# Gate and output projections of a float32 transformer layer in passes of 512 columns, half of them with sums of weight blocks

## The chip, the cores and the metric

The kernel runs on one core of a Trainium2 chip. The metric is device time in microseconds, the median of several executions. Engines are named TensorE (PE in the profile; PEld are its loads of stationary blocks), VectorE (DVE), ScalarE (ACT), GpSimd (POOL) and SyncE (SP, whose queue issues most DMA transfers). A *product* below is one TensorE instruction: a stationary 128 x 128 block of one operand, times a moving block of 128 x 256 of the other, added into a PSUM bank (a bank holds 128 x 512 float32; there are eight).

## The reference

One layer on 256 tokens of width 2048, float32: gated linear attention, then a squared-ReLU MLP, then a last norm. Cut to what matters:

```python
proj = rmsnorm(x, gla_norm) @ w_in                 # q, k, v, r, g_low
q, k, v, r, g_low = split(proj)                    # 1024, 1024, 2048, 2048, 16 columns
o = chunk_causal_linear_attention(q, k, v, gate(g_low))      # 4 heads, chunks of 64
o = o * rsqrt(mean(o * o) + EPS) * o_norm
h = x + (o * silu(r)) @ w_out                      # the gate r and the output projection
a = relu(rmsnorm(h, mlp_norm) @ w_up)
h = h + (a * a) @ w_down
out = rmsnorm(h, final_norm)
```

## The kernel before, in words

**Products.** Every operand of a large projection is split into a high part (rounded to the format that TensorE takes at full rate) and a low part (the rest), and a block product is three products: high x high, high x low, low x high. ScalarE makes high parts (a cast), VectorE low parts (a subtraction). Weights come from memory by SyncE's queue into a raw room, are split into a slot, and are used from there.

**The mixer.** `natural` (line 151) makes a projection for 1024 columns: over 16 blocks of 128 input rows, and both halves of the tokens (t), the stationary block is 128 x 128 of the activations, the moving ones are the weights' columns. That is 24 products a step, 384 a pass, with four banks as sums. `weights` (128) loads and splits one step's 128 x 1024 weights. The order of passes is: values first half, keys, queries (`turned`, 169), values second half (513), gate r first half (568), second half (581), output first half (602), second half (612). `attend` (522) runs beside the first gate pass; `gate_out` (545) multiplies the normed attention output `on` by silu of the gate; `turn` (553) transposes `on` or the new h on TensorE in float32 and splits the result, four times in all: `on` twice, h twice, the last one inside the MLP's plan. `put_v` (336) writes the values' high and low parts out of a pass's banks. Side work is handed out between steps by `pump`, and a scheduler with a timeline model sets the final order of these instructions on each engine.

**Placing of blocks.** The stationary and the moving operand of a product are kept at different places modulo 256 bytes: activations start OFF = 48 words (192 bytes) into a room whose start is a multiple of 256. Behind each group of float32 transposes the kernel runs 24 products whose two operands begin at the same place modulo 256 on purpose (`xe`, `order_of`, the chunks named in SAME, 747).

**The MLP.** Its order is fixed by hand: `at(time, run)` puts steps on a plan whose unit is one product, and the plan is recorded sorted by time (1020). Each *double* is 512 x 512 weights (1 MB). An up double is 48 products. Of the down projection seven eighths go by a scheme in which four block products of a 2 x 2 arrangement are replaced by seven products with sums and differences of blocks: in `raws` (910) 24 products on raw weight blocks, in `summed` (918) 18 on sums of weight blocks, 42 in place of 48. The sums are three adds on VectorE (`adds`, 941), a high part on ScalarE (`high`, 947, two casts) and a low part on VectorE (`low`, 951). One of the sums is made by an accumulating transfer that POOL issues on the raw room (937). The activation side's differences are made by `differ` (798). `combine` (966) adds the pieces up. The chunks' splits are placed by `place_chunks` (717) ahead of their use: a high part 67 to 75 units, a low part 50 to 56 units. All eight banks go round in a list, `banks`.

```python
941        def adds():
943            add(sums[:, 0], view[:, :, 1, left], view[:, :, 0, left])
944            add(sums[:, 1], sums[:, 0], view[:, :, 0, right])
945            sub(sums[:, 2], sums[:, 0], view[:, :, 1, right])
955        at(p - 68, adds)
956        at(q - 74, lambda: high(slice(0, 2)))
958        at(q - 54, low)
959        at(p, lambda: raws(d))
960        at(q, lambda: summed(d))
```

Of the kernel before, what the change touches and what calls it, by code (L numbers as in the profile page):

```python
# [32 lines left out]
P = 128  # L33
# [34 lines left out]
SAME_R = 3  # L68
SAME_O = 3, 3
# [3 lines left out]
def tile_gla_mlp(ctx, tc, x, xt, w_vg, w_in, w_gate, w_out, w_up, w_down, final_norm, out):  # L73
# [6 lines left out]
    mixer = ExitStack()  # L80
    later = mixer.enter_context(tc.tile_pool(name="later", bufs=2))
    mid = mixer.enter_context(tc.tile_pool(name="mid", bufs=1))
    vals = mixer.enter_context(tc.tile_pool(name="vals", bufs=2))
    wpool = mixer.enter_context(tc.tile_pool(name="wpool", bufs=5))
# [199 lines left out]
    h = const.tile([P, NT, D], F32, name="h")  # L284
# [227 lines left out]

    acc = natural(row_x, rows(w_in, 3 * KEYW), G, HALF, order=order_of(SAME_V))
    flush()
    for t in range(NT):
        for c in range(2):
            put_v(acc[t][c], 512, t, G + 512 * c)


    on = later.tile([P, NT, D], F32, tag="C", name="on")  # L520

    def attend(hd, t):
        o = aux_bank()
        blocks = [(0, 0)] if t == 0 else [(0, P), (1, T)]
        vs = slice(hd * DV, (hd + 1) * DV)
        n = 0
        for src, lo in blocks:
            a_h, a_l = (a[hd][:, lo : lo + P] for a in (ath, atl))
            for s, v in ((a_h, vh), (a_h, vl), (a_l, vh)):
                halves(o, s, v[:, src, vs], n == 0, n == 3 * len(blocks) - 1)  # L530
                n += 1
        ss = st.tile([P, 1], F32, tag="oss", name="oss")
        sq = tmp.tile([P, DV], F32, tag="t512", name="sq", bufs=3)
        nc.scalar.activation(sq, o, AF.Square, scale=r1k[:, t : t + 1], accum_out=ss)
        nc.vector.tensor_scalar(ss, ss, 1.0 / DV, EPS, op0=ALU.mult, op1=ALU.add)
# [4 lines left out]
    side.extend([lambda: None] + [lambda hd=hd, t=t: attend(hd, t) for hd in range(HEADS) for t in range(NT)])  # L540


    oth = otl = None

    def gate_out(acc, c0):
        for t in range(NT):
            for c in range(2):
                lo = c0 + 512 * c
                s = tmp.tile([P, 512], F32, tag="t512", name="sr", bufs=3)
                nc.scalar.activation(s, acc[t][c], AF.Silu, scale=r1[:, t : t + 1])  # L550
                nc.vector.tensor_tensor(on[:, t, lo : lo + 512], on[:, t, lo : lo + 512], s, op=ALU.mult)

    def turn(src, row, gain, qs, banks=None):
        banks = banks or [aux_bank(), aux_bank()] + acc_banks(2)
        for q, b in zip(qs, banks):
            for i in range(2):
                kt = 2 * q + i
                for t in range(NT):
                    nc.tensor.transpose(b[:, i * T + t * P : i * T + (t + 1) * P], src[:, t, kt * P : (kt + 1) * P], ident)  # L559
        for n, i, m in ((n, i, m) for n in (0, 2) for i in range(2) for m in range(2)):  # L560
            kt = 2 * qs[n + m] + i
            s = banks[n + m][:, i * T : (i + 1) * T]
            dh, dl = row(kt)
            nc.scalar.activation(dh, s, AF.Copy, scale=gain(kt))
            nc.vector.scalar_tensor_tensor(dl, s, gain(kt), dh.bitcast(F32), op0=ALU.mult, op1=ALU.subtract)


    acc = natural(plain_x, rows(w_in, 4 * KEYW), G, HALF)
    flush()
    gate_out(acc, 0)  # L570
    oth, otl = (vals.tile([P, KT * T + 128], F32R, tag="B", name="ot" + i) for i in "hl")

    def row_o(kt):
        c = kt * T + (OFF if kt < EVEN else 64 if kt == EVEN else OFF + 64)
        return [a[:, c : c + T] for a in (oth, otl)]

    gain_o = lambda kt: go(kt % 4)
    four = lambda *a: [lambda qs=qs: turn(*a, qs) for qs in (range(4), range(4, 8))]
    turns = four(on, row_o, gain_o)
    side.extend([nothing, nothing, turns[0]])  # L580
    acc = natural(row_x, rows(w_in, 5 * KEYW), G, HALF, order=order_of(SAME_R))
    flush()
    gate_out(acc, G)


    side.extend([nothing, nothing, turns[1]])
    hs = const.tile([P, NT, 4], F32, name="hs")

    def add_h(acc, c0):
        for t in range(NT):  # L590
            for c in range(2):
                lo = c0 + 512 * c
                nc.vector.tensor_tensor(h[:, t, lo : lo + 512], acc[t][c], h[:, t, lo : lo + 512], op=ALU.add)

    def ssq_h(c0):
        for t in range(NT):
            for c in range(2):
                lo = c0 + 512 * c
                sq = tmp.tile([P, 512], F32, tag="t512", name="sq", bufs=3)
                nc.scalar.activation(sq, h[:, t, lo : lo + 512], AF.Square, accum_out=hs[:, t, lo // 512 : lo // 512 + 1])  # L600

    acc = natural(row_o, rows(w_out, 0), G, HALF, order=order_of(SAME_O[0]))
    flush()
    add_h(acc, 0)
    hth, htl = (turnp.tile([P, KT * ROW + 64], F32R, tag="A" + i, name="h" + i) for i in "hl")
    turned_h = [hth, htl]
    hth, htl = (a[:, : KT * T].rearrange("p (k t) -> p k t", t=T) for a in turned_h)
    row_h = lambda kt: [a[:, kt, :] for a in (hth, htl)]
    turns = four(h, row_h, g2)
    side.extend([nothing, nothing, turns[0]])  # L610
    side.append(lambda: ssq_h(0))
    acc_o = natural(row_o, rows(w_out, G), G, HALF, order=order_of(SAME_O[1]))
    flush()
    mixer.close()
    mlp = ctx.enter_context(tc.tile_pool(name="mlp", bufs=1, reuse_waits="tile"))

    def room_for(n, name, dtype=F32):
        return mlp.tile([P, n], dtype, tag=name, name=name)

    SLOTS, PLACE = 3, 2 * G + 64  # L620
    raw_u = [room_for(2 * G, f"rawu{i}") for i in range(2)]
    slot = [[room_for(PLACE, f"{x}{i}", F32R) for x in ("high", "low")] for i in range(SLOTS)]
    raw_d = [room_for(2 * G, f"rawd{i}") for i in range(2)]
    sums = room_for(6 * T, "sums").rearrange("p (f b c) -> p f b c", f=3, b=2)
    sums_to = [room_for(6 * T, "sums" + i, F32R).rearrange("p (f b c) -> p f b c", f=3, b=2) for i in "hl"]
    kept = room_for(12 * T, "kept").rearrange("p (c f s) -> p c f s", c=4, f=3)
    flat_forms = room_for(2 * G, "forms")
    forms = flat_forms.rearrange("p (b f s) -> p b f s", b=2, f=8)
    FORMS = 7
    spare = [a[:, KT * T :] for a in turned_h]  # L630
    acts = [
        [
            [(spare[i] if n == b == 0 else room_for(FORMS * P + (OFF if n + b + i == 4 else 64), f"act{n}{b}{i}", F32R))[:, OFF : OFF + FORMS * P] for i in range(2)]
            for b in range(2)
        ]
# [508 lines left out]
```

## Time and profile before

| what | value |
|---|---|
| median of 3 runs | 1048.14 us (1048.13 to 1048.32) |
| the profiled execution | 1048.66 us, of which its span is 1046.9 us |
| granted TensorE clock | 0.999 |
| TensorE busy | 1038.8 us of the span, 9098 instructions |
| VectorE, ScalarE, POOL busy | 811.6, 664.6, 81.7 us |
| read from memory | 206.92 MB, 200 GB/s over the span |

The span is the time from the first to the last instruction that the profiler saw; the execution's own time holds 1.8 us more around it. A line of a group gives source line, engine, operation, output <- inputs, shape and count, then busy time in us and the mean length of one in ns, then the engine's idle time just before such instructions and what ended it. The chain of work is followed back from the last instruction: at each piece to what released it. A matmul's end is modelled, so the distance between starts, which the chain's pieces give, is the better measure of a product's price.

### The profile page before, as it was taken

The page shows a single profiled execution, that of the slowest core. Times are in us where ns is not written, and L with a number is a line of the kernel's source. Part 1 is how long each engine was busy: PE and PEld are TensorE (multiplying, and loading weights), DVE is VectorE, ACT ScalarE, POOL GpSimd, SP SyncE. Part 2 cuts the span into 40 slices and gives each one's busy share as a digit, 9 for nine tenths or more (in the row PEclk, how much of TensorE's full clock was granted, in tenths as well). Part 3 has the DMA queues.
Part 4 walks back from the last instruction along what each step waited for, and adds up shares of the span by engine and source line. Part 5 has one row for each costly group of instructions (what it writes and reads, how often), then busy time and mean ns, then how long its engine had stood idle before and what let it go on. Part 6 is the DMA issues. An engine that isn't in the chain of part 4 may idle for free.

```text
span 1046.9 us, 21360 instructions
## 1 busy us (share of the span) xinstructions
PE 1038.8 (99%) x9098; PEld 1038.6 (99%) x9098; DVE 811.6 (78%) x830; ACT 664.6 (63%) x806; POOL 81.7 (8%) x97
## 2 busy tenths in 40 slices
PE   9999999999999999999999999999999999999997
PEld 9999999999999999999999999999999999999997
DVE  6668654656465566889989989989999999899894
ACT  7675544546455444667677676777767767768763
POOL 0000000010000001010101011010101111010000
PEclk9999999999999999999999999999999999999999
DMA  9857665555655555788878778787788788787662
GB/s 342 309 168 210 195 200 146 177 160 164 200 182 182 202 197 180 224 248 239 231 224 240 225 223 258 214 249 225 226 237 237 212 248 243 203 258 227 195 217 82
DMA packets 108095, 225.08 MB, mean 215 GB/s; under 512 B 6576, under 2 KB 21936, under 8 KB 107872
## 3 DMA queue, kind: packets, MB, share of 16 engines
q1 hardware_dynamic: 91664, 206.75, 60.7%
q0 software_dynamic: 15232, 14.68, 9.0%
q10 hardware_dynamic: 1104, 2.29, 0.6%
q8 instruction: 71, 1.16, 0.4%
q14 instruction: 24, 0.20, 0.0%
HBM read 206.92 MB, written 2.10 MB: 200 GB/s over the span
## 4 chain that ended last, share of the span: by engine, by line
PE 98%; issue 1%; ACT 0%; DVE 0%; POOLq 0%; POOL 0%; ACTq 0%
PE acc L149 28%; PE acc L900 22%; PE aux L774 18%; PE acc L774 16%; PE acc L181 6%; PE aux L900 4%; PE aux L181 2%; PE aux L149 2%; PE aux L216 0%; PE aux L559 0%; PE acc L559 0%; PE acc L473 0%; PE aux L473 0%; ACT sqf L1034 0%; ACT rawd L1102 0%
## 5 line engine op out<-in xcount | busy, mean ns | idle before, releaser
L119 DVE TENSOR_TENSOR lo<-raw,hi 128x1024 fp32r<-128x1024 f32 (+4 forms) x132 | 157.0, 1193 | 126.7 <-ACT hi L118 126.3
L118 ACT CAST hi<-raw 128x1024 fp32r<-128x1024 f32 (+4 forms) x132 | 135.1, 1026 | 150.9 <-PE acc L149 111.8
L738 DVE TENSOR_TENSOR low<-rawu,high 128x2048 fp32r<-128x2048 f32 (+1 forms) x69 | 151.2, 2196 | 10.9 <-ACT high L732 9.2
L774 PE MATMUL aux<-hl,high 128*128 128x256 f32 x544 | 150.3, 276 | 0.0
L774 PE MATMUL aux<-hh,low 128*128 128x256 f32 x544 | 150.3, 276 | 0.0
L774 PE MATMUL aux<-hh,high 128*128 128x256 f32 x544 | 150.3, 276 | 0.0
L949 ACT CAST sumsh<-sums 128x1024 fp32r<-128x1024 f32 x112 | 88.3, 835 | 93.0 <-PE acc L900 72.1
L738 DVE TENSOR_TENSOR low<-rawd,high 128x2048 fp32r<-128x2048 f32 (+1 forms) x59 | 132.7, 2250 | 16.3 <-ACT high L732 16.3
L732 ACT CAST high<-rawd 128x2048 fp32r<-128x2048 f32 (+1 forms) x59 | 111.4, 1890 | 46.8 <-PE acc L774 28.7
L732 ACT CAST high<-rawu 128x2048 fp32r<-128x2048 f32 (+1 forms) x69 | 126.0, 1831 | 20.7 <-PE acc L149 10.5
L774 PE MATMUL acc<-hh,high 128*128 128x256 f32 x480 | 132.8, 277 | 0.0
L774 PE MATMUL acc<-hh,low 128*128 128x256 f32 x480 | 132.6, 276 | 0.0
L774 PE MATMUL acc<-hl,high 128*128 128x256 f32 x480 | 132.6, 276 | 0.0
L900 PE MATMUL acc<-high,act 128*128 128x256 f32 x638 | 121.0, 276 | 0.0
L783 DVE TENSOR_TENSOR sumsl<-sums,sumsh 128x1536 fp32r<-128x1536 f32 x56 | 98.2, 1754 | 25.9 <-ACT sumsh L949 25.9
L937 POOL DMA_DIRECT2D rawd<-rawd x56 | 67.7, 1210 | 514.1 <-DVE sums L925 250.5
L774 PEld LDWEIGHTS aux<-hh,low 128*128 128x128 f32 x544 | 102.2, 188 | 0.0
L774 PEld LDWEIGHTS aux<-hh,high 128*128 128x128 f32 x544 | 102.2, 188 | 0.0
L774 PEld LDWEIGHTS aux<-hl,high 128*128 128x128 f32 x544 | 102.2, 188 | 0.0
L900 PEld LDWEIGHTS acc<-high,act 128*128 128x128 f32 x638 | 101.7, 188 | 0.0
L900 PE MATMUL acc<-sumsh,act 128*128 128x256 f32 x478 | 95.1, 276 | 0.0
L774 PEld LDWEIGHTS acc<-hh,high 128*128 128x128 f32 x480 | 90.2, 188 | 0.0
(251 smaller groups left out, 2603.1 us busy)
## 6 DMA issues: line engine op xcount, KB each, us to landing
rawu<-in_w_up SPq DMA_DIRECT2D x124, 512.0 KB, 4.6
rawd<-in_w_down SPq DMA_DIRECT2D x56, 1024.0 KB, 5.5
raw<-in_w_in SPq DMA_DIRECT2D x80, 512.0 KB, 4.7
raw<-in_w_out SPq DMA_DIRECT2D x32, 512.0 KB, 4.3
rawd<-rawd POOLq DMA_DIRECT2D x56, 256.0 KB, 5.2
rawu<-in_w_down SPq DMA_DIRECT2D x16, 512.0 KB, 4.7
raw<-in_w_vg SPq DMA_DIRECT2D x13, 520.0 KB, 8.1
h<-in_x SPq DMA_DIRECT2D x4, 512.0 KB, 7.1
```

Source lines behind the costliest of these rows:

```text
L118: last_hi[0] = nc.scalar.copy(hi[:, s], raw[:, s])
L119: last_lo[0] = nc.vector.tensor_tensor(lo[:, s], raw[:, s], hi[:, s].bitcast(F32), op=ALU.subtract)
L149: nc.tensor.matmul(o[:, m], x, w[:, m], start=first and c == 0, stop=last, skip_group_check=True)
L181: nc.tensor.matmul(o, u[:, s], m[:, kt], start=kt == 0 and n == 0 and j % 2 == 0, stop=kt == KT - 1 and n == 2, skip_group_check=True,)
L732: nc.scalar.copy(o, i)
L738: nc.vector.tensor_tensor(o, i, x.bitcast(F32), op=ALU.subtract)
L774: nc.tensor.matmul(o, w[:, s], m[:, kt], start=kt == 0 and n == 0 and j % 2 == 0, stop=kt == KT - 1 and n == 2, skip_group_check=True,)
L783: sub = lambda o, x, y: nc.vector.tensor_tensor(o, x, y, op=ALU.subtract)
L900: nc.tensor.matmul(bank[:, o], a[x], w[y], start=fresh and i == 0, stop=d + 1 in starts + [SUMMED] and i == 2, skip_group_check=True,)
L937: nc.gpsimd.dma_start(out=view[:, :, 1, left], in_=view[:, :, 1, right], accum_op=ALU.add)
L949: nc.scalar.copy(sums_to[0][:, f], sums[:, f])
```

## The change

The passes for values, keys and queries stay. Gate and output, before four passes of 1024 columns, become eight passes of 512 columns, four each, named ("r", 0..3) and ("o", 0..3), of four doubles each (512 input rows x 512 columns, 1 MB). A double is either plain (48 products) or with sums (24 + 18). With sums are the doubles of input groups 2 and 3 in the passes r0, r2, o1 and o3, eight in all. All of it goes on the MLP's plan at negative times, ahead of time 0 where the first up double begins, so the order that a scheduler set before is written by hand now. In detail:

- The differences of x blocks that the gate's sums need are made in the values' second pass and kept in h's room, which is taken again for h later (its x is loaded a second time, in time for the output passes). Those of the gated output are made behind its second turn.
- Raw rooms (now three for doubles, a list `raw_u`), slots and sums are taken before the gate passes, in a region at the other end of memory, and stay for the MLP. The MLP's `forms` room is the third raw room.
- The eight attention blocks run inside r0, one after each half of a double. Mean squares are as before, POOL multiplies the factor by r1k in a second step, and ScalarE writes `on`, which VectorE did.
- A pass's sums in banks begin with h copied in by ScalarE (`begin_o`) for the output passes, and end by a copy out (`end_o`) or by `combine_parts`.
- Turns go in groups of 16 transposes with the splits spread over the plan (`put_turned`); the 24 same-place products behind a turn use a copy of two row blocks (`rows_copy`, `again`).
- Banks: one list of eight for all of it. `cleared_bank`, `bank_to_fill` and `bank_in_parts` say what a bank may be used for next.

The core of the diff:

```diff
-    acc = natural(plain_x, rows(w_in, 4 * KEYW), G, HALF)
-    flush()
-    gate_out(acc, 0)
...
-    acc = natural(row_x, rows(w_in, 5 * KEYW), G, HALF, order=order_of(SAME_R))
-    flush()
-    gate_out(acc, G)
...
-    acc = natural(row_o, rows(w_out, 0), G, HALF, order=order_of(SAME_O[0]))
...
-    acc_o = natural(row_o, rows(w_out, G), G, HALF, order=order_of(SAME_O[1]))
+    hbuf = h_tile(F32R)
+    x_forms = {g: sums_of_rows(hbuf[:, OFF + n * 2 * G : OFF + (n + 1) * 2 * G]) for n, g in enumerate((2, 3))}
...
+    for g in (2, 3):
+        side.extend([lambda g=g: x_sums(g), x_differ, lambda g=g: put_sums(x_forms[g], flat(on[:, 0, :])), lambda g=g: put_sums_low(x_forms[g], flat(on[:, 0, :]))])
...
+    def multiply(pc, name, o, a, w, last):
+        b = bank(pc, name)
+        for i, (x, y) in enumerate(((0, 0), (0, 1), (1, 0))):
+            nc.tensor.matmul(b[:, o], a[x], w[y], start=(pc, name) in fresh, stop=last and i == 2, skip_group_check=True)
...
+    def raw_products(p, c, g, last):
+        for b in range(2):
+            w = [x.rearrange("p (b f c) -> p b f c", b=2, f=4)[:, b] for x in parts_of["m", p, c, g]]
+            kt = 4 * g + 2 * b
+            form = lambda f: [sum_forms[p][g][:, n, b, f] for n in range(2)]
+            for f, name, o, a in (
+                (3, B16, left, row_block(p, kt + 1, 0)), (1, T0B, right, row_block(p, kt, 0)),
+                (0, T0B, left, form(S4)), (2, B50, left, form(S1)),
+            ):
+                multiply((p, c), name, o, a, [x[:, f] for x in w], last and b == 1)
+
+    def sum_products(p, c, g, last):
+        for f, name, o in ((0, B16, right), (1, T1B, right), (2, B50, right)):
+            for b in range(2):
...
+                multiply((p, c), name, o, a, [x[:, f, b] for x in sums_to], last and b == 1)
...
+    plain_double("r", 0, 0, between=one_attend)
+    sums_double("r", 0, 2, between=one_attend)
+    plain_double("r", 0, 1, between=one_attend)
+    sums_double("r", 0, 3, between=one_attend)
+    end_of("r", 0)
+    for g in range(4):
+        plain_double("r", 1, g)
+    end_of("r", 1)
+    plain_double("r", 2, 0)
+    sums_double("r", 2, 2)
+    transposes("o0", lambda: on, range(8), "turn o0")
+    plain_double("r", 2, 1, again=True)
+    sums_double("r", 2, 3)
...
+    plain_double("o", 3, 0)
+    sums_double("o", 3, 2)
+    plain_double("o", 3, 1)
+    sums_double("o", 3, 3)
+    end_of("o", 3)
...
+        if not summed_:
+            chunk(key, time - UP_HI, time - UP_LO, time + 2 * UP, (time - UP_EARLY, load), raw)
+            continue
+        chunk(key, time - 67, time - 50, time + RAWS, (time - 165, load), raw)
+        at(time - 116, add_block)
...
+        at(time - 68, adds)
+        at(time - 50, lambda: nc.scalar.copy(sums_to[0][:, :2], sums[:, :2]))
+        at(time - 41, lambda: nc.scalar.copy(sums_to[0][:, 2], sums[:, 2]))
+        at(time - 30, low)
...
-        nc.vector.tensor_scalar(on[:, t, vs], o, r1k[:, t : t + 1], rs, op0=ALU.mult, op1=ALU.mult)
+        nc.gpsimd.tensor_tensor(rs, rs, r1k[:, t : t + 1], op=ALU.mult)
...
+    def attend_put(hd, t):
+        o, rs = attend_state[hd, t]
+        nc.scalar.activation(on[:, t, hd * DV : (hd + 1) * DV], o, AF.Copy, scale=rs)
+        banks.append(o)
+
+    for hd, t, time in attend_at:
+        at(time - LENGTH + 1, lambda hd=hd, t=t: attend_square(hd, t))
+        at(time - LENGTH + 27, lambda hd=hd, t=t: attend_put(hd, t))
```

Here `step` counts products: a plain double advances the plan by 48, one with sums by 24 and 18, and UP_HI, UP_LO, UP_EARLY are 75, 56 and 131 units.

More of the change, by code (lines that the diff above doesn't have):

```diff
@@ L514, in tile_gla_mlp, with room_in @@
     flush()
[L515 to L520, printed above, removed]
+    early.close()
+    zone = ctx.enter_context(tc.tile_pool(name="zone", bufs=1, side="right", reuse_waits="tile"))
+    def room_in(pool, n, name, dtype=F32):
+        return pool.tile([P, n], dtype, tag=name, name=name)
+    SLOTS, PLACE = 3, 2 * G + 64
+    a_slot = lambda i: [room_in(zone, PLACE, f"{x}{i}", F32R) for x in ("high", "low")]
@@ new lines, in tile_gla_mlp, with take_sums @@
+    slot = [a_slot(0)]
+    flat_sums = room_in(zone, 6 * T, "sums")
+    raw_u = [room_in(zone, 2 * G, f"rawu{i}") for i in range(3)]
+    slot += [a_slot(1), a_slot(2)]
+    by_form = lambda a: a.rearrange("p (f b c) -> p f b c", f=3, b=2)
+    sums = by_form(flat_sums)
+    ends = flat_sums[:, : 3 * T].rearrange("p (f s) -> p f s", f=3)
+    sums_to = o_stage = None
+    def take_sums():
+        nonlocal sums_to
+        a = room_in(zone, 12 * T, "sumshl", F32R)
+        sums_to = [by_form(a[:, i * 6 * T : (i + 1) * 6 * T]) for i in range(2)]
@@ new lines, in tile_gla_mlp, with at, chunk, step @@
+    plan = []
+    def at(time, run):
+        plan.append((time, len(plan), run))
+    UP_EARLY, UP_LOAD, UP_HI, UP_LO = 131, 120, 75, 56
+    chunks = []
+    done = set()
+    parts_of = {}
+    banks = []
+    left, right = slice(0, T), slice(T, GT)
+    def chunk(key, hi, lo, end, load, raw):
+        chunks.append((hi, len(chunks), key, lo, end, load, raw))
+    steps, marks, elapsed = [], {}, [0]
+    def step(n, run, mark=None):
+        if mark:
+            marks[mark] = elapsed[0]
+        steps.append((elapsed[0], run))
+        elapsed[0] += n
@@ new lines, in tile_gla_mlp, with plain_double, sums_double @@
+    doubles = []
+    def plain_double(p, c, g, again=False, between=None):
+        doubles.append((p, c, g, False))
+        last = (p, c, g) in LAST_OF
+        for i in range(4):
+            step(12, lambda i=i: plain_rows(p, c, g, i, again, last), ("m", p, c, g) if i == 0 else None)
+            if between and i % 2:
+                between()
+    def sums_double(p, c, g, between=None):
+        doubles.append((p, c, g, True))
+        last = (p, c, g) in LAST_OF
+        step(24, lambda: raw_products(p, c, g, last), ("m", p, c, g))
+        if between:
+            between()
+        step(18, lambda: sum_products(p, c, g, last))
+        if between:
+            between()
@@ new lines, in tile_gla_mlp @@
+    end_of("r", 1)
[4 more added lines that the diff above has]
+    sums_double("r", 2, 3)
+    end_of("r", 2)
+    for g in range(4):
+        plain_double("r", 3, g)
+    end_of("r", 3)
+    plain_double("o", 0, 0)
+    transposes("o1", lambda: on, range(8, 16), "turn o1")
+    plain_double("o", 0, 1, again=True)
+    plain_double("o", 1, 0)
+    plain_double("o", 1, 1)
+    plain_double("o", 0, 2)
@@ new lines, in tile_gla_mlp @@
+    sums_double("o", 1, 2)
+    plain_double("o", 0, 3)
+    end_of("o", 0)
+    sums_double("o", 1, 3)
+    end_of("o", 1)
+    plain_double("o", 2, 0)
+    plain_double("o", 2, 2)
+    transposes("h0", lambda: h, range(8), "turn h0")
+    plain_double("o", 2, 1, again=True)
+    plain_double("o", 2, 3)
+    end_of("o", 2)
+    plain_double("o", 3, 0)
[3 more added lines that the diff above has]
+    end_of("o", 3)
+    LENGTH = elapsed[0]
+    for time, run in steps:
+        at(time - LENGTH, run)
@@ L553, in turn @@
[L553 to L565, printed above, removed]
@@ L613, in tile_gla_mlp @@
[L613 to L624, printed above, removed]
@@ L625, in tile_gla_mlp @@
[L625 to L635, printed above, removed]
-        for n in range(3)
-    ]
@@ new lines, in load_x, with home_h, begin_o @@
+    def load_x(t, half):
+        c = slice(half * G, (half + 1) * G)
+        nc.sync.dma_start(out=h[:, t, c], in_=x[t * P : (t + 1) * P, c])
+    for n, (half, t) in enumerate((half, t) for half in range(2) for t in range(NT)):
+        at(mark("end", "r", 2) + 2 + 8 * n, lambda t=t, half=half: load_x(t, half))
+    def home_h(c, t):
+        return h[:, t, c * GT : (c + 1) * GT]
+    def begin_o(c, t):
+        b = bank_of[("o", c), (T0B, T1B)[t]] = bank_to_fill()
+        nc.scalar.copy(b, home_h(c, t))
@@ L721, in place_chunks @@
             ends.append(end)
-            size = raw.shape[-1]
+            size = 2 * G
             off = OFF if key[0] == "u" else 0
```

430 lines of the change are left out of this document (339 added, 91 removed).

## The prediction

> **What bounds the kernel now.** I read the page first, then what TensorE waited for, then the chain of work in order of time, then busy time by stretch. The page's span, its first table and the shares of the chain:
>
> ```profile
> span 1046.9 us, 21360 instructions
> PE 1038.8 (99%) x9098; PEld 1038.6 (99%) x9098; DVE 811.6 (78%) x830; ACT 664.6 (63%) x806; POOL 81.7 (8%) x97
> PE 98%; issue 1%; ACT 0%; DVE 0%; POOLq 0%; POOL 0%; ACTq 0%
> ```
>
> TensorE's whole list of waits has one line, at the start:
>
> ```profile
> PE aux L216 <- DVE square L213: 1.1, 1, 1.1
> ```
>
> So TensorE, once begun, waits for nobody, and the kernel lasts as long as its products. Busy time overlaps (one product is modelled 276 ns long), so the price of a product is read from the chain, start us, length us, product and count:
>
> ```profile
> 5.69 46.59 PE acc L149 x384
> ...
> 157.98 38.29 PE acc L149 x336
> ...
> 223.47 27.21 PE acc L149 x240
> ...
> 252.42 43.68 PE acc L149 x384
> 297.85 43.67 PE acc L149 x384
> ...
> 378.79 5.44 PE acc L774 x48
> ...
> 435.69 4.76 PE acc L900 x42
> 440.46 5.60 PE aux L774 x48
> ```
>
> 240 gate products take 27.21 us, 48 up products 5.44, 42 down products 4.76: 113.3 ns each wherever the product stands. Two rows are dearer. 384 products after a turn take 43.68 where 384 x 113.3 gives 43.52, and 48 at 440.46 take 5.60 in place of 5.44: in each, 24 products read stationary and moving blocks that begin at the same place modulo 256 bytes, and 0.16 / 24 = 6.7 ns is what that costs a product; elsewhere the stationary block begins 192 bytes on (OFF is 48 words). The first pass, 384 in 46.59, is dear throughout, 121 ns. The program runs 24 same-place products behind every group of float32 transposes; behind them the price is 113.3 again.
>
> **The change, part by part.** *Products.* Eight doubles of weights (two passes of the gate, two of the output, two groups each) go from 48 products to 24 on raw blocks and 18 on sums. TensorE's order in the first gate pass, ahead of the second attention block; before, a row is one stationary block (x: activations) on two halves of the weights' columns:
>
> ```order
> L149 MATMUL acc<-hi,xh 128x256 x4
> L149 MATMUL acc<-lo,xh 128x256 x4
> L149 MATMUL acc<-hi,xl 128x256 x4
> L149 MATMUL aux<-vh,at 128x256 x2
> L149 MATMUL aux<-vl,at 128x256 x2
> ```
>
> and now, in the first double with sums (h is the room where the four differences of x blocks wait):
>
> ```order
> L149 MATMUL aux<-vl,at 128x256 x2
> L149 MATMUL aux<-vh,at 128x256 x2
> L669 MATMUL acc<-high_2349,xh 128x256
> L669 MATMUL acc<-low_2350,xh 128x256
> L669 MATMUL acc<-high_2349,xl 128x256
> L669 MATMUL acc<-high_2349,xh 128x256
> L669 MATMUL acc<-low_2350,xh 128x256
> L669 MATMUL acc<-high_2349,xl 128x256
> L669 MATMUL acc<-high_2349,h 128x256
> L669 MATMUL acc<-low_2350,h 128x256
> ```
>
> Rows of the stream that stood as four column halves now stand as one product of one block; attention, transposes and scores keep their counts. In all TensorE issues 8 x 6 = 48 products fewer: 48 x 113.3 ns = 5.44 us off the path.
>
> *Where the blocks lie.* The differences of x are put 48 words into h's room, and the built program puts h 3,520 bytes into a partition, so they begin at 128 modulo 256; 24 x 4 = 96 products read them as stationary blocks. No row has a distance of 128. The bounds are the two kinds of row above: nothing (distance 192, 113.3 ns) or 6.7 ns (distance 0), 0 to 0.64 us; a gain is excluded, as no row is under 113.3. I take 0.64: 128 is a half of 256 as 0 is a whole of it, while every cheap row is a quarter off. The Trainium skill's page "TensorE: Matmul & The Clock Gate", section "Step-by-step: what each phase is for", says that loading the next weights takes nothing from the running matmul's reads, because TensorE has two SBUF read ports; by it this term is 0, the sum -5.44 and the time 1042.7, the near end of the forecast's own range. The 5.60 us row disagrees with it.
>
> *Sums, and who makes them.* Each double with sums adds on VectorE three adds and one low part, on ScalarE two casts, on POOL an accumulating transfer. The MLP does the same 56 times, so every price is at hand:
>
> ```profile
> L738 DVE TENSOR_TENSOR low<-rawu,high 128x2048 fp32r<-128x2048 f32 x63 | 144.2, 2289 | 10.9 <-ACT high L732 9.2
> L732 ACT CAST high<-rawu 128x2048 fp32r<-128x2048 f32 x63 | 120.1, 1906 | 20.7 <-PE acc L149 10.5 <-DMA rawu<-in_w_up 4.7 <-PE acc L774 4.4
> L783 DVE TENSOR_TENSOR sumsl<-sums,sumsh 128x1536 fp32r<-128x1536 f32 x56 | 98.2, 1754 | 25.9 <-ACT sumsh L949 25.9
> L925 DVE TENSOR_TENSOR sums<-rawd 128x512 f32<-128x512 f32 x56 | 38.3, 684 | 1.2 <-issue 1.2
> L937 POOL DMA_DIRECT2D rawd<-rawd x56 | 67.7, 1210 | 514.1 <-DVE sums L925 250.5 <-DMA rawd<-in_w_down 69.2 <-DVE su L788 61.4
> rawd<-in_w_down SPq DMA_DIRECT2D x56, 1024.0 KB, 5.5
> rawd<-rawd POOLq DMA_DIRECT2D x56, 256.0 KB, 5.2
> ```
>
> VectorE: 2.29 + 3 x 0.68 + 1.75 = 6.1 us in the 4.76 us of such a double, 2.3 in the 5.44 of a plain one: 8.4 in 10.2 when they alternate. Stretches of the gate (first two lines) and of the MLP (last), as us, then PE, PEld, DVE and ACT busy:
>
> ```profile
> 191.00:247.00 56.00, 56.00 (x497) 56.00 (x496) 32.69 (x42) 28.75 (x41) 4.38 (x8) 1.00 0.56 169
> 247.00:297.80 50.80, 50.80 (x450) 50.80 (x449) 27.82 (x31) 24.92 (x32) 0.00 (x0) 1.00 0.58 187
> 600.00:700.00 100.00, 100.00 (x885) 100.00 (x884) 90.12 (x75) 70.99 (x78) 12.08 (x10) 1.00 0.81 236
> ```
>
> In the MLP VectorE works 90.12 of 100 us and TensorE does not wait; the gate has VectorE at 58% of 56 us. The new work fits on average, so I cost it at nothing, provided each piece is ready in its place of a fixed order. That place is tightest in the first gate pass, where ScalarE and POOL carry attention as well. VectorE's order there, before (lo: low parts of weights; vl: values; oss: mean square of an attention block; on: its output):
>
> ```order
> L119 TENSOR_TENSOR lo<-raw,hi 128x1024 x11
> L338 SCALAR_TENSOR_TENSOR vl<-acc,r_122,vh 128x512 x4
> L119 TENSOR_TENSOR lo<-raw,hi 128x1024 x3
> L535 TENSOR_SCALAR oss<-oss 128x1
> L538 TENSOR_SCALAR on<-aux,r1k,ors 128x512
> ```
>
> and now:
>
> ```order
> L1187 TENSOR_TENSOR low_2344<-rawu_2346,high_2343 128x2048
> L344 SCALAR_TENSOR_TENSOR vl<-acc,r_126,vh 128x512 x3
> L519 TENSOR_TENSOR sums<-rawu_2347 128x512
> L519 TENSOR_TENSOR sums<-sums,rawu_2347 128x512
> L520 TENSOR_TENSOR sums<-sums,rawu_2347 128x512
> L344 SCALAR_TENSOR_TENSOR vl<-acc,r_126,vh 128x512
> L1187 TENSOR_TENSOR low_2350<-rawu_2347,high_2349 128x2048
> L885 TENSOR_SCALAR oss<-oss 128x1
> L520 TENSOR_TENSOR sumshl<-sums,sumshl 128x1536
> ```
>
> Sums and low parts now stand between the values and the means; the write of on has left VectorE for ScalarE, behind POOL. On POOL, eight powers in a row have become pairs with the transfers between them:
>
> ```order
> L843 DMA rawu_2347<-rawu_2347 128x2x256
> L314 TENSOR_TENSOR ors<-oss,mhalf 128x1
> L888 TENSOR_TENSOR ors<-ors,r1k 128x1
> L314 TENSOR_TENSOR ors<-oss,mhalf 128x1
> L888 TENSOR_TENSOR ors<-ors,r1k 128x1
> L843 DMA rawu_2346<-rawu_2346 128x2x256
> ```
>
> so the second transfer waits for two attention blocks. I walk this by hand, with the small pieces from:
>
> ```profile
> L338 DVE SCALAR_TENSOR_TENSOR vl<-acc,r,vh 128x512 fp32r<-128x512 f32 x6 | 4.2, 744 | 0.0
> L949 ACT CAST sumsh<-sums 128x1024 fp32r<-128x1024 f32 x56 | 59.1, 1056 | 93.0 <-PE acc L900 72.1 <-PE aux L900 11.5 <-DVE sums L925 7.0
> L949 ACT CAST sumsh<-sums 128x512 fp32r<-128x512 f32 x56 | 34.3, 613 | 0.0
> L534 ACT ACTIVATE sq<-aux,r1k 128x512 f32<-128x512 f32 x8 | 5.5, 684 | 1.5 <-PE aux L149 1.5
> L308 POOL TENSOR_TENSOR ors<-oss,mhalf 128x1 f32<-128x1 f32 x8 | 4.4, 548 | 98.2 <-DVE oss L535 98.2
> L119 DVE TENSOR_TENSOR lo<-raw,hi 128x1024 fp32r<-128x1024 f32 x112 | 136.8, 1223 | 118.3 <-ACT hi L118 118.0
> ```
>
> The value pass ends, and the gate begins, 288 products and 0.16 us after 157.98: 190.8. The first double with sums is due after 48 + 18 products, at 198.3, its sums (24 + 6 on) at 201.7, the second double with sums 126 products after the first, at 212.6. VectorE: three value rows until 192.0, adds until 194.1, the fourth row until 194.8, low part until 197.1, 1.2 us early; its sums' low part until 199, early too. The second: the square of attention block 2 ends about 199.4, POOL's two steps (0.55 each) and hand-overs take until 200.9, the transfer lands 5.2 later, 206.1; adds until 208.2; ScalarE meanwhile casts the high part (1.9) and squares block 4 until 208.8, for whose mean VectorE waits; low part until 211.3, 1.3 us early. So nothing waits, with little over a microsecond to spare. The other six doubles have no attention around them; their low part is placed 50 products (5.7 us) ahead, takes 2.3 and has 3.4 to spare.
>
> *Moved and merged.* The x differences, twelve VectorE steps none longer than the 1.22 us cast, go into the value pass: under 14.7 us, where VectorE has 33.0 - 16.1 free:
>
> ```profile
> 158.00:191.00 33.00, 33.00 (x291) 33.00 (x291) 16.07 (x20) 15.27 (x22) 0.00 (x0) 1.00 0.55 160
> ```
>
> SyncE's weight loads become half as many of 1 MB (5.5 us to land), each asked for 14.8 us or more ahead. h is loaded again between passes; TensorE needs it 20 us later. The four turns keep their 24 same-place products each. MLP and tail keep their order but for which bank is which: nothing, from -0.2 to 0.2.
>
> *Sum.* -5.44 + 0.64 = -4.80. The profiled execution took 1048.66 (span 1046.9), 0.5 above the median, 1048.14; the difference is a count of products and carries over: 1048.14 - 4.80 = 1043.3.
>
> **The rivals.** (1) *Waits in the first gate pass* eat part: 1 to 2.5 us if POOL's transfer lands 2.4 to 3.8 later than 5.2; 1044.4 to 1045.9. For it: margins of 1.2 and 1.3. Against: a late start leaves every later deadline late too.
> (2) *The distance of 128 puts TensorE into the dear regime* of the first pass, until the next 24 same-place products. From the first double with sums to the first turn are 468 products, from the second gate double of that kind to the second turn 296: 764 x 6.7 ns = 5.1 us, gain gone: 1048.14 - 5.44 + 5.1 = 1047.8. Against: same-place products in cheap stretches, the 5.60 row, are followed by cheap ones.
> (3) *Slower: the sums come late at all eight doubles*, because VectorE holds POOL off. Each must cost over 5.44 / 8 = 0.68 us to lose, so transfers must land over 5.2 + 3.4 + 0.68 = 9.3 us after issue at the six roomy doubles; at 10 us: 8 x 1.4 = 11.2, 1048.14 + 5.8 = 1053.9. Against: the MLP's 56 land in 5.2 with VectorE at 90%, and POOL's issue stays at 1.21. The Trainium skill's page "SBUF — State Buffer", section "SBUF: two separate sides", has the rule for it: a transfer issued by POOL starves while VectorE runs an operation that takes the shared port. These rows do not show it.
> (4) *Saved products save nothing*, some other engine bounding: 1048.1. Against: the list of waits.
>
> **How the numbers follow.** Forecast 0.72; rival 1 0.10; rival 2 0.10; rival 3 0.06; rival 4 0.02. About 0.2% (2.1 us) is what a measurement of this kernel can tell from no change. Faster by more: forecast and rival 1, 0.82; within: rivals 2 and 4, 0.12, less 0.01 for a larger loss in rival 2; slower: 0.07. Range: from the whole 5.44 with 0.2 of noise, 1042.5, to past rival 1, 1046.5; that leaves out rivals 2, 3 and 4, 0.18.
>
> **What would show it.** Right: 48 fewer TensorE products, no wait beyond the first, doubles with sums at 4.76 us (4.76 + 12 x 6.7 ns = 4.84 in the gate), plain ones 5.44. Rival 1: TensorE waits for low or high of the second or fourth double. Rival 2: plain gate doubles at 5.7 us. Rival 3: waits for sums, low after low. A span over 1048 with no wait listed would refute the whole count.

## The result, and the profile after

| kernel | median | executions | ratio to before |
|---|---|---|---|
| before | 1048.05 us | 1047.8 to 1048.32, 6 | |
| after | 1055.91 us | 1054.93 to 1056.8, 6 | 1.0075 [1.0062, 1.0088] |

The change makes the kernel 7.9 us slower where 4.8 us faster was forecast. The page of after, its span, first table and chain:

```profile
span 1055.0 us, 21250 instructions
PE 1039.9 (99%) x9050; PEld 1037.9 (98%) x9050; DVE 848.1 (80%) x856; ACT 690.3 (65%) x824; POOL 101.7 (10%) x113
PE 85%; DVE 5%; DMA 4%; ACT 3%; issue 2%; POOL 1%; SPq 0%; POOLq 0%; ACTq 0%; DVEq 0%
```

The 48 products are gone (9098 to 9050), yet the span has grown by 8.1 us, and a chain that was TensorE's for 98% now runs for a seventh over other engines. TensorE's list of waits (us in total, times, longest):

```profile
PE acc L669 <- DVE low L1187: 4.2, 3, 2.4
PE aux L669 <- DVE low L1187: 1.8, 1, 1.8
PE aux L216 <- DVE square L213: 1.1, 1, 1.1
PE aux L669 <- ACT on L893: 0.5, 1, 0.5
PE acc L149 <- DVE h L519: 0.5, 1, 0.5
```

The chain in order of time (start us, length us, what) says where they come from:

```profile
200.43 0.17 DVE oss L885
200.67 2.52 POOL ors L314
...
203.79 6.93 DMA rawu<-rawu
...
213.64 2.54 POOL ors L314
...
226.39 1.80 ACT high L1181
...
234.33 1.90 ACT high L1181
...
238.57 5.03 DMA rawu<-in_w_in
...
244.16 7.70 DMA rawu<-rawu
...
286.46 17.11 PE acc L669 x143
```

From 189 to 286 us no piece of it is TensorE's. POOL's power, 0.55 us in the profile of before, takes 2.5 here, and the transfer that stands behind it on POOL lands 6.9 us later. The eight such transfers have a median of 6.8 where the MLP's have 5.2, but a median says little of one of them: the 56 in before took from 3.6 to 8.5 us.

```profile
rawu<-rawu POOLq DMA_DIRECT2D x8, 256.0 KB, 6.8
```

This one went out at 203.79, 0.94 us behind a weight load of 1 MB that SyncE had issued:

```profile
202.85 0.37 SPq L840 DMA_DIRECT2D rawu<-in_w_in  x1
203.79 1.21 POOL L843 DMA_DIRECT2D rawu<-rawu  x1 [0.33 <-issue]
```

Why the power takes so long is seen beside VectorE's timeline (start, length, line, tile; in brackets the idle time ahead):

```profile
200.50 2.28 DVE L1187 TENSOR_TENSOR low<-rawu,high 128x2048 fp32r<-128x2048 f32 x1
204.88 0.15 DVE L885 TENSOR_SCALAR oss<-oss 128x1 f32<-128x1 f32 x1 [2.10 <-ACT sq L884]
210.80 0.69 DVE L519 TENSOR_TENSOR sums<-rawu 128x512 f32<-128x512 f32 x1 [5.76 <-DMA rawu<-rawu]
```

and POOL's:

```profile
196.81 1.93 POOL L314 TENSOR_TENSOR ors<-oss,mhalf 128x1 f32<-128x1 f32 x1 [11.38 <-DVE oss L885]
...
200.67 2.52 POOL L314 TENSOR_TENSOR ors<-oss,mhalf 128x1 f32<-128x1 f32 x1 [1.66 <-DVE oss L885]
...
205.13 0.56 POOL L314 TENSOR_TENSOR ors<-oss,mhalf 128x1 f32<-128x1 f32 x1
```

The power that starts at 200.67 ends at 203.19, 0.41 us behind the end of VectorE's low part; the one at 205.13, with VectorE idle, takes 0.56. The other four long powers (at 196.81, 213.64, 218.17 and 222.20) also end 0.40 to 0.42 us behind a VectorE instruction with two operands in SBUF, and so do the six of late_on_a. Before, VectorE itself wrote `on` and so stood idle for the power. The Trainium skill's page "SBUF — State Buffer", section "SBUF: two separate sides", has this under "Who interferes with whom": VectorE with two SBUF operands and a GpSimd operation that reads SBUF exclude each other for a whole instruction. The trace agrees, with the 0.41 us; the prediction took only that section's remark on transfers, whose issue took 1.21 us here too.

Busy time by stretch (us, then PE with its count of products, PEld, DVE, ACT, POOL, the granted clock, DMA):

```profile
217.00:219.00 2.00, 2.00 (x12) 2.00 (x11) 1.07 (x2) 2.00 (x4) 0.83 (x1) 0.50 0.93 266
226.00:236.00 10.00, 10.00 (x86) 10.00 (x86) 6.67 (x11) 8.23 (x11) 1.48 (x4) 1.00 0.60 207
```

A stretch also counts the products that it cuts at its ends. In the first the clock stands at 0.50, as it does for 3.4 us from 216.8 on, one microsecond after the longest stop ended, and a product takes 213 ns. The second lies in a gate pass that reads no block at a distance of 128, and still its products are dear: 117.8 ns by the distance between their starts, where the same pass had 113.3 before. The dear price sets in before any stop: it is 113.3 up to 198.9 us, and from the first double that reads blocks at a distance of 128 (the first such product starts at 198.98) it is 117.8. Nearly all of the loss can be read from the starts of TensorE's products. From 190.5 to 304 us there are five stops (2.69, 0.80, 2.12, 0.76, 1.57 from start to start), 7.4 us beyond the products in them; 0.5 in the product behind each (some 222 ns); 1.5 at half clock; 3.05 in dear products beyond the 0.3 of the turns; and one more stop near the end, 0.74. Together 13.2 of the 13.5 us by which the span exceeds 1046.9 - 5.44.

### The profile page after: what moved, and what is told of

Same layout as the page of the kernel before. It is cut to its first block, busy times and chain, and to the rows that moved or that the text cites. A ratio compares the mean times of both kernels' runs of the same rounds, so it can differ in the third digit from the quotient of the medians.

```text
span 1055.0 us, 21250 instructions
## 1 busy us (share of the span) xinstructions
PE 1039.9 (99%) x9050; PEld 1037.9 (98%) x9050; DVE 848.1 (80%) x856; ACT 690.3 (65%) x824; POOL 101.7 (10%) x113
## 4 chain that ended last, share of the span: by engine, by line
PE 85%; DVE 5%; DMA 4%; ACT 3%; issue 2%; POOL 1%; SPq 0%; POOLq 0%; ACTq 0%; DVEq 0%
PE acc L1223 29%; PE acc L1343 17%; PE acc L149 8%; PE acc L669 8%; PE aux L1343 7%; PE acc L181 6%; PE aux L1223 4%; DVE low L1187 2%; PE aux L181 2%; DMA raw<-in_w_vg 1%; DMA rawu<-rawu 1%; PE aux L669 1%; ACT high L1181 1%; POOL ors L314 1%; DMA rawu<-in_w_down 1%
## 5 line engine op out<-in xcount | busy, mean ns | idle before, releaser
L1223 PE MATMUL acc<-hh,high 128*128 128x256 f32 x896 | 247.6, 276 | 0.0
L1223 PE MATMUL acc<-hh,low 128*128 128x256 f32 x896 | 247.5, 276 | 0.0
L1223 PE MATMUL acc<-hl,high 128*128 128x256 f32 x896 | 247.5, 276 | 0.0
L1223 PEld LDWEIGHTS acc<-hh,low 128*128 128x128 f32 x896 | 168.3, 188 | 0.0
L1223 PEld LDWEIGHTS acc<-hl,high 128*128 128x128 f32 x896 | 168.3, 188 | 0.0
L1392 ACT CAST sumshl<-sums 128x1024 fp32r<-128x1024 f32 x112 | 88.3, 834 | 93.0 <-PE acc L1343 61.1
L520 DVE TENSOR_TENSOR sumshl<-sums,sumshl 128x1536 fp32r<-128x1536 f32 x64 | 112.3, 1754 | 26.5 <-ACT sumshl L1392 25.4
L1343 PE MATMUL acc<-high,acts 128*128 128x256 f32 x510 | 101.7, 276 | 0.0
L1343 PEld LDWEIGHTS acc<-high,acts 128*128 128x128 f32 x510 | 83.6, 188 | 0.0
L1343 PE MATMUL acc<-sumshl,acts 128*128 128x256 f32 x600 | 80.7, 276 | 0.0
```

The source lines that it names most:

```text
L520: sub = lambda o, x, y: nc.vector.tensor_tensor(o, x, y, op=ALU.subtract)
L1223: nc.tensor.matmul(o, w[:, s], row_h(kt)[m], start=kt == 0 and n == 0 and j % 2 == 0, stop=kt == KT - 1 and n == 2, skip_group_check=True,)
L1343: nc.tensor.matmul(bank[:, o], a[x], w[y], start=fresh and i == 0, stop=d + 1 in starts + [SUMMED] and i == 2, skip_group_check=True,)
L1392: nc.scalar.copy(sums_to[0][:, f], sums[:, f])
```

## The experiments

Medians, and the ratio to before, measured beside each. Distances go modulo 256 bytes from the place of the moving block, the shorter way round: the differences of x lie 192 bytes on in quarter, a distance of 64, and 224 on in late_32, a distance of 32.

| run | edit to after (stall: to before) | median us | ratio |
|---|---|---|---|
| quarter | differences of x at distance 64 | 1056.50 | 1.0082 [1.0067, 1.0097] |
| on_v | VectorE writes `on` | 1048.85 | 1.0012 [1.0002, 1.0022] |
| both | the two | 1049.65 | 1.0013 [1.0003, 1.0022] |
| sums_o | no sums in the gate | 1048.03 | 0.9995 [0.9986, 1.0005] |
| late_silu | both, silu later | 1043.39 | 0.9955 [0.9939, 0.9970] |
| late_again | the same again | 1043.09 | 0.9954 [0.9942, 0.9967] |
| late_128 | the same, distance 128 | 1047.09 | 0.9990 [0.9980, 1.0000] |
| late_0 | the same, distance 0 | 1044.37 | 0.9964 [0.9952, 0.9976] |
| late_32 | the same, distance 32 | 1046.94 | 0.9987 [0.9978, 0.9996] |
| late_on_a | the same, `on` as in the change | 1052.65 | 1.0038 [1.0025, 1.0051] |
| stall | one wait in the MLP | 1057.36 | 1.0110 [1.0024, 1.0196] |
| stall_same | and same-place products behind | 1049.84 | 1.0016 [1.0007, 1.0026] |

**quarter.**

```diff
-    ... hbuf[:, OFF + n * 2 * G : OFF + (n + 1) * 2 * G] ...
+    ... hbuf[:, n * 2 * G : (n + 1) * 2 * G] ...
```

> Only the place of the differences of x changes: they begin 192 in place of 128 bytes into a stretch of 256, as all other stationary blocks do. In the profile after, some 690 more products than before take about 120 ns in place of 113.3, 690 x 6.7 ns = 4.6 us. Theory (dear products hidden under waits): the chain between 190 and 286.5 us runs over POOL, DMA, ScalarE and VectorE and not over TensorE, so TensorE leaves its last wait there at the same time as now; what is gained is only the 141 dear products behind it, 0.95 us: 1055.0, all of the gate's products at 113.3 ns, and the listed waits grow by about 3.6 us. Rival (the two losses add up): 1055.9 - 4.6 = 1051.3, waits as now. If the distance has nothing to do with the price: 1055.9 and still products of 120 ns.

1056.50: nothing gained, 1.5 over the first theory and 5.2 over the rival. The waits grew as expected:

```profile
PE acc L669 <- DVE low L1187: 4.6, 2, 2.7
PE aux L669 <- DVE low L1187: 1.9, 1, 1.9
...
PE acc L669 <- ACT high L1181: 1.0, 1, 1.0
PE aux L669 <- ACT on L893: 0.5, 1, 0.5
```

but the expectation of 113.3 ns throughout failed. Stretches of the gate, ahead of the first stop and behind the later ones:

```profile
191.00:211.00 20.00, 20.00 (x179) 20.00 (x178) 9.10 (x11) 9.72 (x15) 6.80 (x7) 1.00 0.42 119
226.00:236.00 10.00, 10.00 (x86) 10.00 (x86) 6.67 (x11) 8.22 (x11) 1.48 (x4) 1.00 0.60 207
```

With every block at a quarter's distance, products were cheap until TensorE stopped, and dear from then on up to the next turn. A stop is a second way into the dear price; this run, meant for another question, was the first to show it.

**on_v.**

```diff
         rsqrt(rs, ss)
-        nc.gpsimd.tensor_tensor(rs, rs, r1k[:, t : t + 1], op=ALU.mult)
+        nc.vector.tensor_scalar(on[:, t, ...], o, r1k[:, t : t + 1], rs, op0=ALU.mult, op1=ALU.mult)
...
-        nc.scalar.activation(on[:, t, ...], o, AF.Copy, scale=rs)
```

> VectorE writes the normed attention output again, directly behind the mean square, in place of ScalarE, and POOL's second step goes; VectorE then waits for POOL's power, so no long VectorE work runs beside it. Theory (POOL's power, 0.55 us when VectorE is idle, takes 1.9 to 2.5 while VectorE works, and that lateness runs on through transfer, high and low parts): all eight powers take 0.55, the second transfer of the gate goes out 2.5 us earlier, and most of the 7.4 us of waits go; dear products stay: 1055.9 - 6.5 = 1049.4, waits under 1 us in all. Rival (the transfer's landing of 7 us and the weights' rooms make the waits, POOL's power does not): over 1053.5, waits for low parts at the same four places.

1048.85, near the 1049.4 of the theory. In after, the group of eight powers stands as

```profile
L314 POOL TENSOR_TENSOR ors<-oss,mhalf 128x1 f32<-128x1 f32 x8 | 13.2, 1651 | 30.7 <-DVE oss L885 30.6
```

and here as

```profile
L314 POOL TENSOR_TENSOR ors<-oss,mhalf 128x1 f32<-128x1 f32 x8 | 4.4, 552 | 33.3 <-DVE oss L885 33.3
```

The first gate pass has no wait left; 1.7 us remain later, more than the microsecond that was expected, and the dear products. The second transfer now goes out ahead of SyncE's load:

```profile
200.04 1.21 POOL L843 DMA_DIRECT2D rawu<-rawu  x1
203.17 0.37 SPq L840 DMA_DIRECT2D rawu<-in_w_in  x1
```

It lands 3.6 us after issue, as it does within 0.1 us in all seven traces where it goes first; in the three where the load goes first (after, quarter, late_on_a) it takes 6.6 to 7.4. So the late landing comes with the late power; no run changed that order alone.

**both.** The two edits together.

> The differences of x at 192 bytes and the attention output written by VectorE, together. Theory: both losses go, what is left is the forecast of 1043.3 and a wait of 0.64 us near the end, 1043.9; up to 1045.5 if TensorE, now faster, meets low parts that are up to 1.5 us late. So the two edits together give 12 us, the one alone 1 and the other alone 6.5. Rival (there is a third cause that no row shows yet): over 1047.

1049.65, no better than on_v alone: the rival was right, there is a third cause. The waits of this run:

```profile
PE acc L669 <- DVE low L1186: 2.5, 2, 1.9
...
PE aux L669 <- DVE low L1186: 0.8, 1, 0.8
PE acc L149 <- DVE h L519: 0.4, 1, 0.4
```

ScalarE's timeline ahead of the first of them:

```profile
222.53 0.73 ACT L964 ACTIVATE sr<-sr,r 128x512 f32<-128x512 f32 x1 [1.62 <-DVE sr L519]
225.57 0.72 ACT L964 ACTIVATE sr<-sr,r 128x512 f32<-128x512 f32 x1 [2.32 <-DVE sr L519]
226.20 5.51 ACT L1180 CAST high<-rawu 128x2048 fp32r<-128x2048 f32 x3
```

The two silu of the pass just ended wait for VectorE's combination, and three high parts of the next pass's weights queue behind them. The chain ahead of the stop at 278 us also runs from a silu to a high part to a low part; the one at 248 us follows from the first, through loads that wait for raw rooms. Stretches ahead of the stop at 229 us and behind it:

```profile
207.00:227.00 20.00, 20.00 (x179) 20.00 (x178) 16.64 (x21) 11.13 (x16) 2.20 (x4) 1.00 0.50 164
231.00:246.00 15.00, 15.00 (x129) 15.00 (x129) 6.20 (x7) 3.23 (x4) 2.43 (x2) 1.00 0.81 239
```

179 products in 20 us are cheap, 129 in 15 (172 in 20) dear.

**sums_o.** The gate's `sums_double` calls become `plain_double`, its ends those of plain passes.

> The gate's four doubles with sums are made plain (48 products each), all else stays: only o1 and o3 have sums, 24 products fewer than before. Theory: without transfers and sums in the gate and without blocks at 128 bytes neither loss is left: 1048.05 - 24 x 113.3 ns = 1045.3, and 0.64 of the wait near the end, 1046.0. Rival (passes of 512 columns on a schedule written by hand cost by themselves, attention on ScalarE among it): 1049 or more, with waits in the first gate pass though there are no sums.

1048.03, between the two: not the 1046.0 of the theory, nor the 1049 and the waits in the first gate pass of the rival. TensorE's list has

```profile
PE acc L669 <- DVE low L1187: 0.3, 1, 0.3
```

and by starts two more hesitations, about 10 ns at 220 us and 0.08 us at 232.0, each followed by 117.8 ns, the latter up to the turn at 254. (Whether the 10 ns are the cause of the change at 220 us or a part of it is not shown.) Between them, behind the listed wait at 226 us, the products took 113.3 again. These stops and 237 dear products cost 1.8 us; before's span less 24 products plus this, 1046.9 - 2.72 + 1.8 = 1046.0, stands against a span of 1045.7. The stop of 0.08 us cost its length ten times over: some 190 products x 4.44 ns.

**stall and stall_same.** To the kernel before, a wait of a known kind; in stall_same, 32 joins the chunks in SAME.

```diff
+            if u == 32 and i == 0:
+                b = group_banks[g][0][:, :P]
+                nc.tensor.matmul(b, wh[:, :P], hth[:, kt, :P], start=True, stop=True, skip_group_check=True)
+                seen = tmp.tile([P, P], F32R, tag="t512", name="seen", bufs=3)
+                nc.scalar.copy(seen, b)
+                nc.tensor.matmul(b, wh[:, :P], seen, start=True, stop=True, skip_group_check=True)
...
-    SAME = (1, 4, LEAD + 1, LEAD + 2)
+    SAME = (1, 4, LEAD + 1, LEAD + 2, 32)
```

> The kernel before, with one wait of TensorE put into the middle of the MLP: ahead of up double 32 TensorE makes one small product, ScalarE copies it out, and TensorE makes a second one that reads the copy; both are overwritten. About 3,300 products follow without any group of same-place products. In the traces so far a wait of TensorE among cheap products (113.33 ns) was followed by dear ones (117.78 ns) five times in six, up to the next 24 same-place products. Theory (a wait can change the price of all that follows): the wait itself, 0.5 to 3 us, and 3,300 x 4.44 ns = 14.7 us in most executions: 1063 to 1066, single executions at 1049 to 1051 possible, nothing between. Rival (a wait costs its length): 1049 to 1051 in every execution, 113.33 ns behind it.

> The same wait, and the first 24 products behind it (the first half of up double 32) read stationary and moving blocks that begin at the same place modulo 256 bytes, as behind the kernel's float32 transposes. Theory (same-place products set the price back): 0.5 to 3 us of wait and 24 x 6.7 ns = 0.16 us, then 113.33 ns to the end: 1049 to 1051.2 in every execution. Rival (only what follows float32 transposes is set back by them): as the run without them, 1063 to 1066.

Four executions of stall: 1049.64, 1050.1, 1064.62 and 1064.92, nothing between. Two paid the wait alone, two 15 us more, as 3,300 x 4.44 ns would give. The profiled execution was one of the first kind, with 113.3 ns behind the wait, so that the other two had dear products is inferred from this size; the two added products in it:

```profile
664.57 0.22 PE L772 MATMUL aux<-hh,high 128*128 128x128 f32 x1
666.23 0.33 PE L775 MATMUL aux<-seen,high 128*128 128x128 f32 x1 [1.44 <-ACT seen L774]
```

Ten executions of stall_same lie between 1049.63 and 1050.38: 24 same-place products set the price back without float32 transposes ahead of them too. In stall the dear kind came in two of four; among all stops in cheap products of the gate's and the tail's traces, in most. In sums_o a stop in dear products was followed by cheap ones. So a stop does not always set the price dear, it draws it anew; what decides the draw no run shows.

**late_silu.** To both, three steps moved later, the silu, the last part of the combination and the loads of h:

```diff
-        for n, run in ((-11, first), (-6, second), (1, third)):
+        for n, run in ((-11, first), (-6, second), (42 if p == "r" else 1, third)):
...
-            at(e + 4 + 8 * t, silu)
-            at(e + 11 + 8 * t, times)
+            at(e + 46 + 8 * t, silu)
+            at(e + 53 + 8 * t, times)
...
-        at(mark("end", "r", 2) + 2 + 8 * n, lambda t=t, half=half: load_x(t, half))
+        at(mark("end", "r", 2) + 30 + 24 * n, lambda t=t, half=half: load_x(t, half))
```

> The kernel with both edits, and the silu of the passes with sums, the last part of their combination and the loads of h are placed 4 to 5 us later, so that the high parts of the weights behind a gate pass stand ahead of them on ScalarE. Theory (the three waits left, 0.9, 0.7 and 2.1 us with what they do to the price behind them, come from high parts that stood in order behind a silu which waits for VectorE): no wait is left in the gate, all its products at 113.33 ns, and the time is the forecast of 1043.3, or 1044.0 to 1044.5 where the wait near the end (0.66 us and dear products behind it) comes too. Rival (the waits come from loads and transfers that land late): over 1047, waits at the same places.

1043.39, and 1043.09 in the second measurement, late_again:

> The kernel with all three edits (differences of x at 192 bytes, attention output on VectorE behind its mean, silu and loads of h later) once more, for its interval: 1043.4, from 1042.5 to 1044.6 by how late three of the last weights' loads land (the wait of 0.3 to 0.7 us near the end), 4 to 5 us faster than before.

No wait is left in the gate. The second gate pass in late_silu's chain, and a long piece behind the first turn:

```profile
218.79 21.76 PE aux L669 x192
...
252.50 37.56 PE acc L669 x330
```

192 products at 113.3 ns, 330 at 113.8, 24 of these same-place ones behind the turn.

**late_128, late_0, late_32.** late_silu with the differences of x moved: `OFF`, 16 or 8 words into h's room, at distances of 128, 0 and 32 bytes from the moving blocks.

> As the kernel with the later silu, but with the differences of x at 128 bytes, as the change has them: the distance alone, without waits. Theory (a few products at this distance put TensorE into the dear price until the next same-place group): 764 products dearer by 4.44 to 6.7 ns, 3.4 to 5.1 us over the later silu: 1046.7 to 1048.4 if that is 1043.3. Rival (only the 96 products themselves are dearer): 0.64 us over it.

> As the kernel with all three edits, but the differences of x begin at the same place modulo 256 as the moving blocks (distance 0), where the change has a distance of 128. If a distance of 128 acted as a distance of 0 does, which is what the term of 0.64 us in the sum assumed, this would cost what the distance of 128 did, 3.7 us: 1047.1. Theory (same-place products are dearer themselves, 6.7 ns each, but leave the price behind them cheap): 96 x 6.7 ns = 0.64: 1044.0, products behind them at 113.3.

> As the kernel with all three edits, but with a distance of 32 bytes between the differences of x and the moving blocks, which no run has shown. If only a distance of 128 (a half) brings the dear price: 1043.4. If every distance but 64 and 192 does, as far as it isn't 0: 1047.

The same pass of late_128:

```profile
219.65 22.61 PE aux L669 x192
```

of late_0:

```profile
219.84 21.76 PE aux L669 x192
```

and of late_32:

```profile
219.53 22.61 PE aux L669 x192
```

None of these 192 products reads a difference; those that did came earlier. Behind distances of 128 and 32 they take 117.8 ns, behind 0 and 64 they take 113.3. The medians follow: 3.7 and 3.9 us over late_silu and late_again for 128 and 32; 1.3 for 0, of which the same-place products explain 0.64. The wait near the end, 0.5 in the profiled execution and followed by dear products, may be the rest; its share of the median is not shown. The dear price begins at the first double that reads a difference, at 198 us, in both late_128 and late_32.

**late_on_a.** late_silu with `on` written by ScalarE behind POOL.

> As the kernel with all three edits, but the attention output is written by ScalarE behind two steps of POOL, as the change has it: POOL's stretched power alone. Theory (the power runs beside VectorE's low parts again, 1.9 to 2.5 us in place of 0.55 in most of the eight): the first gate pass waits for the low part of its second double with sums, 3 to 4.5 us; behind a wait that long 1.6 us at half the clock; some 400 dear products up to the first turn, 1.8 us: 1043.4 + 6.4 to 7.9 = 1049.8 to 1051.3. Rival (the order of high parts and silu on ScalarE was the whole cause): 1044.5 or less.

1052.65, 9.6 over late_again and 1.35 over the theory's upper end. The powers, and the first waits:

```profile
L314 POOL TENSOR_TENSOR ors<-oss,mhalf 128x1 f32<-128x1 f32 x8 | 15.2, 1896 | 30.5 <-DVE oss L885 30.3
```

```profile
PE acc L669 <- DVE low L1187: 2.7, 1, 2.7
...
PE aux L669 <- DVE low L1187: 0.9, 2, 0.7
PE aux L669 <- ACT on L893: 0.5, 1, 0.5
```

The wait came where it was expected, and the products behind it were dear; the clock stayed at 1.00 behind it, against the expectation, and later stops, which it did not have, made up for that.

## Why the prediction was wrong, point by point

**Products**: right. 9050 in place of 9098, and with all three obstacles gone the kernel saves 4.8 and 5.3 us against the before measured beside it, of the 5.44 counted. The saving was there and was overdrawn. That these times, 1043.1 to 1043.4, also match the forecast of 1043.3 is partly luck: the 0.64 us in that sum belongs to blocks at a distance of 128, which this kernel does not have, and a wait of 0.2 to 0.5 us near the end stands in its place.

**Where the blocks lie**: mis-sized. The term took 128 to act as 0 does, 0.64 us for 96 products. It acts otherwise: the products behind them are dear, 3.7 us. Rival 2 had the mechanism and was given 0.10, because same-place products are followed by cheap ones; but those are the products that set the price back, so the 5.60 us row said nothing about 128. Rival 2's price of 6.7 ns was too high: 4.44 at a distance of 64. The dear price was on record in the first pass of before: its 121 ns mix 96 products of 272 columns with 288 of 256, whose starts lie 118 ns apart in the median. By the rule of the Trainium skill's page "TensorE: Matmul & The Clock Gate", section "Step-by-step: what each phase is for", that weight loads take nothing from the running product's reads, the term would be nothing; 3.7 us is farther from that than the prediction thought. What in TensorE makes the price depend on the place no run shows.

**Sums, and who makes them**: this step failed. It cost the new work at nothing, by a walk through the first gate pass that took POOL's power at 0.55 us from rows in which VectorE was idle, though the changed order puts a low part or a sum right behind the mean. The first power took 1.9, so the square of block 2 ended at 200.4 in place of 199.4. The second took 2.5, and from the square to the transfer's issue it was 3.4 us in place of 1.5. The transfer, now behind SyncE's load, took 6.9 in place of its median of 5.2 (3.6 where it goes first) and landed at 210.7 in place of 206.1, against margins of 1.2 and 1.3. That is rival 1's place, with a lateness of 4.6 where it allowed 3.8. And the lateness did not end there: it went on through ScalarE's order (silu ahead of high parts), the raw rooms and the next loads to three more stops. "A late start leaves every later deadline late too" holds only if the late engine catches up while TensorE stands.

**Moved and merged** at nothing: the move of `on` from VectorE to ScalarE, with POOL's second step, which took away VectorE's idle time beside POOL, costs 9.6 us by itself (late_on_a); the place of the silu on ScalarE, of the combination's last part and of the loads of h 6.3 together (both to late_silu); the distance 3.7. How the 6.3 divide was not tried; that the silu is the main part is argued from the chain alone. They sum to 19.6 where the change lost 12.8 to the kernel without them, because waits hide dear products and each other: quarter gained nothing, on_v 7.1.

**A wait's price**: missing from the sum and from every rival. All counted a wait at its length. It also draws the price of what follows, up to the next same-place products.

**The slower rival**, sums late at all eight doubles, gave 1053.9 for another reason than came true: the four doubles of the output passes never waited. It had the right pair of engines, since VectorE did hold POOL off, but in its powers and not in the issue of its transfers. **The tail** was costed at up to 0.2 and had a wait of 0.74 in after by starts; the last weights' loads take up to 8.9 us to land there, up to 6.6 in before, though asked for in the same order. The traces of on_v, sums_o and late_128 show no such wait. Why the loads land later was not tried and stays open.

## What to carry to other kernels

Take an operation's duration only from a row in which its neighbours are busy as they will be, and when work leaves an engine, ask who profited from the idle time that it left. A stop of a saturated TensorE can cost far more than its length, so a deadline with a microsecond to spare in a chain over three engines and a transfer is not met until a run shows it. A late start can also put a transfer behind a bigger one, and so grow on its way. Repair one loss at a time only with an eye on the others: here the first repair measured nothing and the last one everything.

## What the runs showed of the hardware

- A product of 128x256 costs 113.33 ns or 117.78 at a distance of 64, for hundreds or thousands of products on end. Blocks at distances of 128 and 32 led into the dear price in every trace that has them, a stop of TensorE from 0.08 us up may, 24 same-place products (about 120 ns each) led out of it.
- A power on POOL of one element a partition takes 0.55 us beside an idle VectorE, and 1.9 to 2.5 beside its two-operand work; all eleven such powers of after and late_on_a ended 0.40 to 0.42 us behind VectorE's instruction.
- The second accumulating transfer of the gate, 256 KB from POOL, landed in 3.6 to 3.7 us where it was issued ahead of a weight load of 1 MB (seven traces), and in 6.6 to 7.4 where it was issued behind it (three).
- After the 2.69 us stop in after, and one of 3.06 in quarter, with one of 1.27 a product ahead of it, the clock was granted at 0.50 for 3.4 us; after one of 2.95 in late_on_a (all from start to start) it was not. The Trainium skill's page "TensorE: Matmul & The Clock Gate", section "Part 1: The HAM clock gate", has half clock after an idle window of about 3.4 us; here all these stops are shorter, and the longer of the two single ones did not bring it.
